# An encoder block on one core: table copies six behind each matmul group and an earlier table load; norm 2, transposes and row sums at fixed steps of the output projection

## The chip, the core and the metric

The kernel runs on one core of a Trainium2 chip. The metric is the device time of one execution in microseconds (us): the median of several runs. The engines of the core work side by side, each through its own list of instructions in order: TensorE (PE in the profile; PEld is its weight load), VectorE (DVE), ScalarE (ACT), GpSimd (POOL) and SyncE (SP, which here only issues DMAs; ACT issues a few as well). They wait for one another by semaphores.

## What is computed

One layer of an encoder block on 1024 tokens of 1024 channels, all in float32:

```python
h = rms_norm(x, norm1_g[l])
z = h @ w_in[l]                                   # 1024 -> 2560
a, gate, q, k, v = jnp.split(z, splits, axis=-1)  # 512 each
conv_out = conformer_conv(a, gate, ...)           # GLU, 31 taps, layer norm, swish
q, k = rms_norm(q), rms_norm(k)                   # per head of 64
attn_out = neighbourhood_attention(q, k, v, rpb[l])
x = x + jnp.concatenate([conv_out, attn_out], axis=-1) @ w_out[l]
h = rms_norm(x, norm2_g[l])
x = x + (jax.nn.silu(h @ w_gate[l]) * (h @ w_up[l])) @ w_down[l]   # 1024 -> 2816 -> 1024
```

The attention is over a grid of 16 rows by 64 columns: each query looks at 8 rows by 16 columns around it, clamped inside the grid, with a learned bias `rpb` by head, row offset and column offset.

## The kernel before

**Products.** A float32 product is made as three TensorE passes over operands that are split into a high and a low part (`split`, line 102: ACT casts the high part, DVE or POOL subtracts it for the low part; `mac`, line 109: high by high, high by low, low by high, lines 111 to 113). A tile of 128 tokens (or 128 features) by 512 takes 8 steps of three matmuls, one for each 128 channels.

**Order by hand.** The order of each engine's list is the order in which the Python program emits instructions. Between two steps of a product, `weave()` (line 118) takes one function off the list `woven` and calls it, so that a transpose or an evacuation lands between two steps; `unravel()` empties the list. In the first half of the kernel, `step()` (line 397) stands after each product of 24 matmuls: it calls `behind()` (line 479), which issues the next few jobs of the list `aside_dma`, then the postponed evacuation of the product before, some taps of the convolution on DVE (`pump`) and one on ACT and POOL (`side`).

**First half.** Keys (8 tiles, `wk`), GLU of the convolution (16 tiles, `gl`), queries (8 tiles, `z` from `w00` to `w03`), values (8 tiles, `z` from `w20` to `w23`). Weights are loaded by SP into three rotating buffers (`issue`, line 133, whose DMAs bear line 140) and split into their place (`take`). A value tile is copied out of PSUM by ACT and stored to DRAM, `vd` (`value_out`, line 389); windows of it come back as `vw` (`load_vw`, line 561).

**Tables.** The bias of the attention is laid out in DRAM by copies (`bias_tables`, line 444), 102 jobs in this order: for each of three types of column window, 16 runs of `rpb` into `t1` (line 461; `t<-in_rpb` in the profile) and two fills of `tf` with a very negative number (line 456; `tf<-neg`, three or four DMAs each); then 48 copies of rows from `t1` to `tf` (line 467; `tf<-t`). The list is set up after key tile 4, and from key tile 5 on each step issues four. After value tile 3 what is left is issued, and the first three tables are loaded (`table`, line 545; `tab<-tf`, line 554). The first table goes to three buffers of 1024 columns, the others to large ones that held the transposed input.

**Attention.** 32 steps, each of two heads: scores (`s`, line 581), bias and row maximum on DVE (line 594), exponential on ACT, division on POOL, transposes (`p`, line 612), product with the values (`o`, line 628). Scores of step 0 stand after value tile 5, those of step 1 after tile 6; scores and tiles share four PSUM banks.

**Output projection and norm 2.** The second column half of the output projection is made for t = 0 to 7 (lines 924 to 944, tile `pk`). After each tile: residual on DVE (`resid`, line 735), then `norm2` (line 807): store of the row to `xd`, square with sum and square root on ACT, reciprocal and product on DVE into `xn`. Of the first four tiles, `norm_T` transposes the eight channel blocks into `h2`, 3 + 2 + 3 of them woven into the products of tiles 5, 6 and 7. `t_sums` (line 832) and `s_sum` (line 882) make the sums of weight blocks and of token halves that the next stage needs; `prep` (line 848) splits the weights.

**FFN.** Gate and up projection are made as a two-by-two block scheme with seven products (m1 to m7) in place of eight, each of 4 steps, in the order m1, m2, m6, m5, m7, m4, m3 for the first two feature tiles (lines 1084 to 1091, `product` and `evac`). Its operands on the token side are A11 and A12 (from `h2`), and S1 to S4 and A22, which `s_T` (line 896) transposes from sums (`sn`) or rows (`xn`), 4 blocks each, into two PSUM tiles of 512 (`sq`, `sr`) and the two halves of one of 1024 (`sp`), and splits. `s_weave` (line 911) weaves them into the products ahead of the one that reads them. POOL makes the sums for S3 and S4 (`s_sum` with (3, 4)).

Of the kernel before, what the change touches and what calls it, by code (L numbers as in the profile page):

```python
# [7 lines left out]
F32R = mybir.dt.float32r  # L8
AF = mybir.ActivationFunctionType
# [3 lines left out]
P = 128  # L13
D = 1024
S = 1024
KB = D // P
# [50 lines left out]
def build(ctx, tc, a):  # L67
    nc = tc.nc
    pe, act, dve, pool = nc.tensor, nc.scalar, nc.vector, nc.gpsimd
# [14 lines left out]
    def H(name, dt=F32):  # L84
        return T("H", [P, 4096], 6, name, dt)
# [4 lines left out]
    def SM(name, n=8):  # L90
        return T("sm", [P, 8], 16, name)[:, :n]

    def mm(name):
        return ps.tile([P, 512], F32, tag="mm", bufs=4, name=name)

    def tp(name):
        return ps.tile([P, 512], F32, tag="tp", bufs=2, name=name)

    def cv(name):
        return ps.tile([P, 1024], F32, tag="cv", bufs=1, name=name)  # L100

    def split(hi, lo, src, sub=(pool,)):
        act.copy(hi, src)  # L103
        n = src.shape[-1] // len(sub)
        for i, eng in enumerate(sub):
            sl = slice(i * n, (i + 1) * n)
            eng.tensor_tensor(*[w[..., sl] for w in (lo, src, hi.bitcast(F32))], OP.subtract)  # L107
# [8 lines left out]
    woven = []  # L116
# [104 lines left out]
    ident = T("ident", [P, P], 1, "ident")  # L221
    ones = ST("ones")[:, :P]
    eps = T("eps", [P, 1], 1, "eps")
# [12 lines left out]
    def rstd_of(ss, scale, name):  # L236
        n = ss.shape[-1]
        sd = SM(name + "d", n)
        act.activation(sd, ss, AF.Sqrt, bias=eps, scale=scale)
        r = SM(name + "r", n)  # L240
        dve.reciprocal(r, sd)
        return r
# [4 lines left out]
    def norm_T(xs, g, dst, o, tag, lag=0, per=1, gap=0, spare=False, kbs=range(KB)):  # L247
        n = len(xs) * P

        def one(kb):  # L250
            pt = (mm if spare and kb % 3 else tp)(f"{tag}{kb}")[:, :n]
            for i, xt in enumerate(xs):
                pe.transpose(pt[:, i * P:(i + 1) * P], xt[:, kb * P:(kb + 1) * P], ident)
            hi, lo = dst[0][:, kb, o:o + n], dst[1][:, kb, o:o + n]
            if g is None:
                split(hi, lo, pt, (dve,))
            else:
                act.activation(hi, pt, AF.Copy, scale=g[:, kb:kb + 1])
                dve.scalar_tensor_tensor(lo, pt, g[:, kb:kb + 1], hi.bitcast(F32), OP.mult, OP.subtract)
        woven.extend([lambda: None] * lag)  # L260
        for k0 in range(0, len(kbs), per):
            woven.append(lambda k0=k0: [one(kbs[k0 + i]) for i in range(per)])
            woven.extend([lambda: None] * gap)
# [212 lines left out]
            for rh in range(2):  # L476
                aside_dma.extend(lambda rh=rh, ty=ty, i=i: rows_of(rh, ty, i) for i in range(8))

    def behind(n=4):
        for _ in range(n):  # L480
            if aside_dma:
                aside_dma.pop(0)()
# [62 lines left out]
    def table(rh, ty):  # L545
        n = AR * t1[ty].shape[-1]
        src = tf[rh, ty].rearrange("i j h c -> (i j) (h c)")
        if rh == 0 and ty == 0:
            parts = [(G(f"tab{k}")[:, :n * min(3, NH - 3 * k)], 3 * k) for k in range(3)]
        else:  # L550
            parts = [(H(f"tab{rh}{ty}")[:, :NH * n], 0)]
        heads = []
        for w, h0 in parts:
            nc.sync.dma_start(w, src[:, h0 * n:h0 * n + w.shape[-1]])
            heads += [w[:, o:o + n] for o in range(0, w.shape[-1], n)]
        return heads
# [90 lines left out]

    for t in range(6):
        value(t)
        if t == 3:  # L650
            while aside_dma:
                behind()
            tab[0, 0] = table(0, 0)
            tab[1, 0] = table(1, 0)
            tab[0, 3] = table(0, 2)
    pump(200)
# [17 lines left out]
    cm, x2, xn = [], {}, {}  # L674
# [69 lines left out]
    for i in range(2, 32 + 2):  # L744
# [8 lines left out]
        if i < 32:  # L753
            ss = score_mm(i)
# [45 lines left out]
    for t in range(6, 8):  # L800
# [3 lines left out]
        take(2)  # L804
        resid(t, 0, acc0[t])

    def norm2(t):
        nc.sync.dma_start(xd[t * P:(t + 1) * P, :], x2[t])
        ss = SM(f"s2{t}", 1)
        act.activation(cv(f"jk{t}"), x2[t], AF.Square, accum_out=ss)  # L810
        r = rstd_of(ss, 1.0 / D, f"r2{t}")
        xn[t] = G(f"xn{t}")
        dve.scalar_tensor_tensor(xn[t], x2[t], r, g2b, OP.mult, OP.mult)

# [6 lines left out]
    HK, QF = KB // 2, FB // 2  # L821
    raw_gu, top, tsum = {}, {}, {}

    def load_gu(i, j):
        if i < FB:
            raw_gu[i, j] = R(f"gu{i}{j}")
            nc.sync.dma_start(raw_gu[i, j], a["gu"][ms[i], j])

    def lr(w):
        return w[:, :512], w[:, 512:]  # L830

    def t_sums(i, ns):
        (b11, b21), (b12, b22) = lr(raw_gu[i, 0]), lr(raw_gu[i, 1])
        for n in ns:
            if n in (1, 3):
                tsum[i, n // 2] = G(f"ts{i}{n}")
            o = lr(tsum[i, (n - 1) // 2])[(n - 1) % 2]
            l, r = ((b12, b11), (b22, lr(tsum[i, 0])[0]), (b22, b12), (b21, lr(tsum[i, 0])[1]))[n - 1]
            dve.tensor_tensor(o, l, r, OP.subtract)  # L839
# [37 lines left out]


    h2 = []
    sn, sop, slot = {}, {}, []  # L880

    def s_sum(t, ns, eng):
        (x11, x12), (x21, x22) = lr(xn[t]), lr(xn[t + 4])
        for n in ns:
            if n == 1:
                sn[t] = G(f"sn{t}")
            s1, s2 = lr(sn[t])
            o, l, r, op = ((s1, x21, x22, OP.add), (s2, s1, x11, OP.subtract),
                           (x21, x11, x21, OP.subtract), (x12, x12, s2, OP.subtract))[n - 1]
            eng.tensor_tensor(o, l, r, op)  # L890

    def s_rows(n, t):
        return {"S1": lambda: sn[t][:, :512], "S2": lambda: sn[t][:, 512:], "S3": lambda: xn[t + 4][:, :512],
                "S4": lambda: xn[t][:, 512:], "A22": lambda: xn[t + 4][:, 512:]}[n]()

    def s_T(n, kb):
        if kb == 0:
            if n == "S4":
                q = [lr(G(f"S4{i}", F32R)) for i in range(HK)]
                sop[n] = [[w[h] for w in q] for h in range(2)]  # L900
            else:
                q = H(n, F32R).rearrange("p (w k s) -> p w k s", w=2, s=512)
                sop[n] = [[q[:, h, i] for i in range(HK)] for h in range(2)]
        if not slot:
            slot.extend([tp("sq"), tp("sr"), *lr(cv("sp"))])
        pt = slot.pop(0)
        for t in range(4):
            pe.transpose(pt[:, t * P:(t + 1) * P], s_rows(n, t)[:, kb * P:(kb + 1) * P], ident)
        split(sop[n][0][kb], sop[n][1][kb], pt, (dve,))

    def s_weave(n):
        if n == "S2":
            skip = lambda: None
            s2 = [lambda kb=kb: s_T(n, kb) for kb in range(HK)]
            woven.extend([skip, skip, s2[0], skip, s2[1], s2[2], s2[3]])
            return
        for kb in range(HK):
            woven.extend([lambda n=n, kb=kb: s_T(n, kb), lambda: None])

    g2b = G("g2b")  # L920
    nc.sync.dma_start(g2b, a["g2"].to_broadcast([P, D]))
    for i, j in ((0, 0), (0, 1), (1, 0)):
        load_gu(i, j)
    for t in range(8):
        acc = mm(f"pk{t}")
        proj(t, 1, acc, (4, 5, 6, 7, 0, 1, 2, 3))
        unravel()
        if t == 4:
            h2 += [H(f"h2{w}", F32R).rearrange("p (k s) -> p k s", s=512) for w in range(2)]
        if 4 <= t < 7:  # L930
            norm_T([xn[i] for i in range(4)], None, h2, 0, "t20", 3, gap=1,
                   kbs=((0, 1, 2), (3, 4), (5, 6, 7))[t - 4])
        if t == 7:
            s_sum(2, (1, 2), dve)
        resid(t, 1, acc)
        norm2(t)
        if t in (1, 2):
            t_sums(0, (2 * t - 1, 2 * t))
        if t in (3, 4):
            prep()  # L940
        if t in (5, 6):
            s_sum(t - 5, (1, 2), dve)
        if t == 5:
            prep()
    act.activation(warm, eps, AF.Silu)
    s_sum(3, (1, 2), dve)
    prep()
# [136 lines left out]
    for n, (i, p) in enumerate(products):  # L1084
        if i == 0 and p in NEXT:
            s_weave(NEXT[p])
        acc = product(i, p)
        if 2 <= n < 6:
            s_sum(n - 2, (3, 4), pool)
        evac(i, p, acc)  # L1090
        if late and p != "m4":
            late.pop(0)()
        if extra and p in ("m2", "m5", "m7", "m6"):
            extra.pop(0)()
        prep()
        if i == FB - 1 and p in ("m2",):
            for q in range(4):
                load_item(q)
        if i == FB - 1 and p in ("m5", "m7", "m3", "m4"):
            prep_items(1)  # L1100
# [53 lines left out]
    for s, p in enumerate(SEQ):  # L1154
        for k in range(QF - 2):
            n = s * QF + k
# [34 lines left out]
```

## Time and profile before

| | us |
|---|---|
| median of 3 runs | 1104.6 |
| the runs | 1103.31 to 1105.61 |
| the profiled execution | 1105.57 |
| its span, from the first to the last instruction | 1103.8 |

All lines of the profile, and all durations below, are of the one profiled execution. The numbers at the head of a line of a timeline are the start, in us from the start of the span, and the duration; then engine, line of the kernel, operation, written and read tiles, shapes and the number of instructions merged (x). A q behind the engine stands for its queue: the line tells when DMAs were issued, not when they landed. In brackets stands how long the engine was idle before, and what ended that.

### The profile page before, as it was taken

Reading aid. Unit: us, or ns where it says so; the run is one execution under the profiler, and the core shown is the slowest. Engines: PE = TensorE matmul, PEld = TensorE weight load, DVE = VectorE, ACT = ScalarE, POOL = GpSimd, SP = SyncE. Lnnn points to the kernel's source line nnn. Section 1 sums busy time; section 2 is a strip of 40 time slices with the busy share of each in tenths; the row PEclk is TensorE's granted clock in tenths of the full one; section 3 lists DMA queues with packets and bytes.
Section 4 is the critical chain, followed back from the end, with each engine's and each line's share of the span. In section 5 each row is a group of like instructions: output and inputs, shape, how many; then the busy total and the mean of one; then the engine's idle time right before and its main releaser. Section 6 shows DMA issues by size and latency. Waiting matters only on the chain.

```text
span 1103.8 us, 14180 instructions
## 1 busy us (share of the span) xinstructions
PE 1066.7 (97%) x5124; PEld 855.1 (77%) x5124; DVE 692.2 (63%) x1033; ACT 449.8 (41%) x1061; POOL 390.6 (35%) x303
## 2 busy tenths in 40 slices
PE   5999999997999999899999999999999999999997
PEld 4888888874657788678888888888888888888886
DVE  6557987782675425756465655646465577757883
ACT  5656336613776523542323222222322345433441
POOL 4025573501454122444544544454454300002220
PEclk9999999998999999999999999999999999999999
DMA  7004473046621552113313223322322479533651
GB/s 301 26 24 150 148 246 96 5 135 220 185 91 56 131 158 96 42 54 117 112 67 136 101 88 106 119 101 72 137 97 86 162 278 340 183 96 115 187 163 42
DMA packets 65495, 139.87 MB, mean 127 GB/s; under 512 B 12305, under 2 KB 18961, under 8 KB 64785
## 3 DMA queue, kind: packets, MB, share of 16 engines
q1 hardware_dynamic: 63584, 135.75, 37.2%
q10 hardware_dynamic: 1840, 3.22, 0.8%
q8 instruction: 40, 0.66, 0.2%
q14 instruction: 31, 0.25, 0.1%
HBM read 99.80 MB, written 44.76 MB: 131 GB/s over the span
## 4 chain that ended last, share of the span: by engine, by line
PE 88%; DVE 4%; ACT 3%; DMA 2%; issue 1%; SPq 1%; POOL 1%; ACTq 0%; DVEq 0%
PE B L111 5%; PE B L113 5%; PE B L112 5%; PE D L111 4%; PE D L113 4%; PE D L112 4%; PE z L111 3%; PE z L113 3%; PE z L112 3%; PE A L111 3%; PE A L113 3%; PE A L112 3%; PE gl L111 3%; PE gl L112 3%; PE gl L113 2%; PE p L612 2%
## 5 line engine op out<-in xcount | busy, mean ns | idle before, releaser
L314 DVE SCALAR_TENSOR_TENSOR cv<-u,par,cv 128x1009 f32<-128x1009 f32 (+11 forms) x96 | 122.7, 1278 | 2.8
L107 DVE TENSOR_TENSOR op<-sr,op 128x512 fp32r<-128x512 f32 x77 | 59.3, 770 | 15.5 <-ACT op L103 15.3
L103 ACT CAST op<-sr 128x512 fp32r<-128x512 f32 x77 | 47.6, 618 | 50.5 <-PE B2d L113 20.9
L340 POOL TENSOR_TENSOR pa<-pa,pr 128x1022 f32<-128x1022 f32 (+4 forms) x20 | 48.0, 2398 | 56.2 <-ACT pr L339 52.4
L978 DVE TENSOR_TENSOR g<-B,g 128x512 f32<-128x512 f32 x22 | 15.2, 691 | 80.3 <-PE B L113 80.3
L1146 POOL TENSOR_TENSOR ou<-ou,resm 128x512 f32<-128x512 f32 x8 | 13.3, 1665 | 141.8 <-DMA resm<-xd 141.2
L987 ACT ACTIVATE D<-D 128x512 f32<-128x512 f32 x22 | 12.8, 582 | 114.5 <-DVE D L986 114.5
L603 POOL TENSOR_SCALAR e<-e,rs 128x288 f32<-128x288 f32 (+1 forms) x64 | 34.0, 544 | 67.4 <-PE s L581 38.5
L973 DVE TENSOR_TENSOR u<-B,g 128x512 f32<-128x512 f32 x22 | 15.2, 691 | 65.2 <-PE B L113 65.2
L103 ACT CAST op<-wd 128x512 fp32r<-128x512 f32 x66 | 40.9, 619 | 33.0 <-DVE wd L1065 18.3
L107 DVE TENSOR_TENSOR op<-wd,op 128x512 fp32r<-128x512 f32 x66 | 51.7, 783 | 2.7 <-ACT op L103 1.1
L839 DVE TENSOR_TENSOR ts<-gu,ts 128x512 f32<-128x512 f32 x44 | 52.1, 1184 | 0.8
L976 ACT ACTIVATE A<-A 128x512 f32<-128x512 f32 x20 | 11.6, 582 | 77.4 <-PE A L113 77.4
L596 ACT ACTIVATE e<-e,mx 128x288 f32<-128x288 f32 (+1 forms) x64 | 36.2, 568 | 16.0 <-DVE mx L594 16.0
L594 DVE CUSTOM_DVE_ANT_0 e<-s,tab 128x288 f32<-128x288 f32 (+1 forms) x64 | 29.8, 503 | 16.6 <-DMA tab<-tf 8.4
L612 PEld LDWEIGHTS p<-ident,e 128*96 128x96 f32 (+1 forms) x192 | 20.4, 135 | 19.0 <-issue 10.7
L839 DVE TENSOR_TENSOR ts<-gu 128x512 f32<-128x512 f32 x22 | 34.2, 1553 | 0.0
L581 PE MATMUL s<-kT,qT 64*128 64x288 f32 (+1 forms) x128 | 28.6, 509 | 5.4 <-DVE mx L594 5.4
L612 PE MATMUL p<-ident,e 128*96 128x128 f32 (+1 forms) x192 | 28.1, 284 | 3.9 <-DVE pT L617 2.5
L628 PE MATMUL o<-pT,vw 96*64 96x128 f32 (+1 forms) x384 | 28.6, 283 | 1.7 <-DMA vw<-vd 1.7
L362 ACT ACTIVATE sq<-z 128x64 f32<-128x64 f32 x128 | 26.4, 247 | 8.4 <-PE z L113 8.4
L628 PEld LDWEIGHTS o<-pT,vw 96*64 96x64 f32 (+1 forms) x384 | 20.6, 138 | 7.9 <-issue 5.8
(1072 smaller groups left out, 3486.0 us busy)
## 6 DMA issues: line engine op xcount, KB each, us to landing
gu<-in_gu SPq DMA_DIRECT2D x44, 512.0 KB
sr<-sd SPq DMA_DIRECT2D x77, 256.0 KB
sd<-sd SPq DMA_DIRECT2D x22, 512.0 KB
wd<-in_wd SPq DMA_DIRECT2D x44, 256.0 KB
sd<-g SPq DMA_DIRECT2D x33, 256.0 KB
x<-in_x SPq DMA_DIRECT2D x16, 512.0 KB
xd<-x SPq DMA_DIRECT2D x8, 512.0 KB
resm<-xd SPq DMA_DIRECT2D x16, 256.0 KB
```

Source lines behind the costliest of these rows:

```text
L103: act.copy(hi, src)
L107: eng.tensor_tensor(*[w[..., sl] for w in (lo, src, hi.bitcast(F32))], OP.subtract)
L111: pe.matmul(acc, lh, rh, start=start, stop=False, skip_group_check=True)
L112: pe.matmul(acc, lh, rl, start=False, stop=False, skip_group_check=True)
L113: pe.matmul(acc, ll, rh, start=False, stop=stop, skip_group_check=True)
L314: dve.scalar_tensor_tensor(acc[:, o], uc[:, i], dwk[:, c, t:t + 1], acc[:, o], OP.mult, OP.add)
L340: pool.tensor_tensor(pa[:, o], pa[:, o], pr[:, o], OP.add)
L596: act.activation(e[:, hh], e[:, hh], AF.Exp, bias=mx, scale=-1.0, accum_out=rs[:, hh:hh + 1])
L603: pool.tensor_scalar(es[i][:, hh], es[i][:, hh], rs[:, hh:hh + 1], 1.0, op0=OP.mult, op1=OP.mult)
L612: pe.transpose(pt[:m, g * P:(g + 1) * P], es[i][:, hh, g * m:(g + 1) * m], ident)
L628: pe.matmul(os_[s_][hh * HD:(hh + 1) * HD, hp], vw[cb, rh + g][:, c:c + HD], pTs[i][:, g, hh], start=g == 0, stop=g == 2)
L839: dve.tensor_tensor(o, l, r, OP.subtract)
```

## The change

- `behind` issues six jobs in place of four.
- The remaining jobs and the first table's load stand after value tile 2 and not 3; the other two tables stay after tile 3.
- `norm2` is cut in two: store, square and root stay after the tile; reciprocal and product (`norm2_out`) stand at step 4 of the next tile.
- The transposes into `h2` stand at fixed steps: blocks 0, 1, 2 at steps 0, 2, 5 of tile 5, blocks 3, 4, 5 at the same steps of tile 6, blocks 6 and 7 at steps 0 and 1 of tile 7. `h2` is allocated ahead of the loop.
- `t_sums` of the first weights move from behind tiles 1 and 2 to step 5 of tiles 2 and 3; the row sums from behind tiles 5 and 6 and ahead of residual 7 to steps 1 of tile 6, and 2 and 6 of tile 7.
- `s_T` takes three parts for an operand: blocks 0 and 1 each to a tile `sq`, blocks 2 and 3 together to the two halves of `sp`, split by one ACT and one DVE instruction of 1024 columns (S4: by two each).
- POOL's sums: one per product behind products 1 to 8, first the four for S3, then the four for S4, in place of two behind each of products 2 to 5.

```diff
-    def behind(n=4):
+    def behind(n=6):
...
     for t in range(6):
         value(t)
-        if t == 3:
+        if t == 2:
             while aside_dma:
                 behind()
             tab[0, 0] = table(0, 0)
+        if t == 3:
             tab[1, 0] = table(1, 0)
             tab[0, 3] = table(0, 2)
...
         ss = SM(f"s2{t}", 1)
         act.activation(cv(f"jk{t}"), x2[t], AF.Square, accum_out=ss)
-        r = rstd_of(ss, 1.0 / D, f"r2{t}")
+        sd2[t] = SM(f"r2{t}d", 1)
+        act.activation(sd2[t], ss, AF.Sqrt, bias=eps, scale=1.0 / D)
+
+    def norm2_out(t):
+        r = SM(f"r2{t}r", 1)
+        dve.reciprocal(r, sd2[t])
         xn[t] = G(f"xn{t}")
         dve.scalar_tensor_tensor(xn[t], x2[t], r, g2b, OP.mult, OP.mult)
...
-        pt = slot.pop(0)
-        for t in range(4):
-            pe.transpose(pt[:, t * P:(t + 1) * P], s_rows(n, t)[:, kb * P:(kb + 1) * P], ident)
-        split(sop[n][0][kb], sop[n][1][kb], pt, (dve,))
+        two = kb == 2
+        pt = cv("sp") if two else tp("sq")
+        for j in range(1 + two):
+            for t in range(4):
+                pe.transpose(pt[:, j * 512 + t * P:j * 512 + (t + 1) * P],
+                             s_rows(n, t)[:, (kb + j) * P:(kb + j + 1) * P], ident)
+        if two and n != "S4":
+            split(*[w[:, kb:kb + 2].rearrange("p k s -> p (k s)") for w in sop[n, "all"]], pt, (dve,))
+        else:
+            for j in range(1 + two):
+                split(sop[n][0][kb + j], sop[n][1][kb + j], lr(pt)[j] if two else pt, (dve,))
 
     def s_weave(n):
...
+        skip = lambda: None
+        parts = [lambda kb=kb: s_T(n, kb) for kb in range(3)]
+        woven.extend([skip, skip, parts[0], skip, parts[1], parts[2]] if n == "S2" else
+                     [parts[0], skip, parts[1], skip, parts[2]])
...
+    beside = {t: {4: [lambda t=t: norm2_out(t - 1)]} for t in range(1, 8)}
+    for t in (2, 3):
+        beside[t][5] = [lambda t=t: t_sums(0, (2 * t - 3, 2 * t - 2))]
+    for t, s, kbs in ((5, 0, (0, 1, 2)), (6, 0, (3, 4, 5)), (7, 0, (6, 7))):
+        for n, kb in enumerate(kbs):
+            at_ = n if t == 7 else 2 * n + (n == 2)
+            beside[t].setdefault(at_, []).append(lambda kb=kb: t2_one(kb))
+    beside[6].setdefault(1, []).append(lambda: s_sum(0, (1, 2), dve))
+    beside[7].setdefault(2, []).append(lambda: s_sum(1, (1, 2), dve))
+    beside[7].setdefault(6, []).append(lambda: s_sum(2, (1, 2), dve))
+
+    def t2_one(kb):
+        mark = len(woven)
+        norm_T([xn[i] for i in range(4)], None, h2, 0, "t20", kbs=(kb,))
+        woven.pop(mark)()
+
     for t in range(8):
+        for n in range(KB):
+            woven.append(lambda fs=beside.get(t, {}).get(n, ()): [f() for f in fs])
         acc = mm(f"pk{t}")
         proj(t, 1, acc, (4, 5, 6, 7, 0, 1, 2, 3))
         unravel()
-        if t == 4:
-            h2 += [H(f"h2{w}", F32R).rearrange("p (k s) -> p k s", s=512) for w in range(2)]
-        if 4 <= t < 7:
-            norm_T([xn[i] for i in range(4)], None, h2, 0, "t20", 3, gap=1,
-                   kbs=((0, 1, 2), (3, 4), (5, 6, 7))[t - 4])
-        if t == 7:
-            s_sum(2, (1, 2), dve)
         resid(t, 1, acc)
         norm2(t)
-        if t in (1, 2):
-            t_sums(0, (2 * t - 1, 2 * t))
-        if t in (3, 4):
+        if t in (3, 4, 5):
             prep()
-        if t in (5, 6):
-            s_sum(t - 5, (1, 2), dve)
-        if t == 5:
-            prep()
+    norm2_out(7)
     act.activation(warm, eps, AF.Silu)
     s_sum(3, (1, 2), dve)
     prep()
...
-        if 2 <= n < 6:
-            s_sum(n - 2, (3, 4), pool)
+        if 1 <= n < 9:
+            s_sum((n - 1) % 4, (3 + (n > 4),), pool)
```

More of the change, by code (lines that the diff above doesn't have):

```diff
@@ L805, in build @@
         resid(t, 0, acc0[t])
+    sd2 = {}
     def norm2(t):
@@ L879, in build @@
     h2 = []
-    sn, sop, slot = {}, {}, []
+    sn, sop = {}, {}
     def s_sum(t, ns, eng):
@@ L903, in s_T @@
                 sop[n] = [[q[:, h, i] for i in range(HK)] for h in range(2)]
-        if not slot:
-            slot.extend([tp("sq"), tp("sr"), *lr(cv("sp"))])
-        pt = slot.pop(0)
-        for t in range(4):
-            pe.transpose(pt[:, t * P:(t + 1) * P], s_rows(n, t)[:, kb * P:(kb + 1) * P], ident)
-        split(sop[n][0][kb], sop[n][1][kb], pt, (dve,))
-    def s_weave(n):
[L912 to L918, printed above, removed]
+                sop[n, "all"] = [q[:, h] for h in range(2)]
+        two = kb == 2
[9 more added lines that the diff above has]
+                split(sop[n][0][kb + j], sop[n][1][kb + j], lr(pt)[j] if two else pt, (dve,))
+    def s_weave(n):
+        skip = lambda: None
+        parts = [lambda kb=kb: s_T(n, kb) for kb in range(3)]
+        woven.extend([skip, skip, parts[0], skip, parts[1], parts[2]] if n == "S2" else
+                     [parts[0], skip, parts[1], skip, parts[2]])
     g2b = G("g2b")
@@ L923, in build @@
         load_gu(i, j)
+    h2 += [H(f"h2{w}", F32R).rearrange("p (k s) -> p k s", s=512) for w in range(2)]
+    beside = {t: {4: [lambda t=t: norm2_out(t - 1)]} for t in range(1, 8)}
[12 more added lines that the diff above has]
+        woven.pop(mark)()
     for t in range(8):
+        for n in range(KB):
+            woven.append(lambda fs=beside.get(t, {}).get(n, ()): [f() for f in fs])
         acc = mm(f"pk{t}")
```

## The prediction

> **What bounds the kernel now.** I read the page first, then the waits of TensorE, then the two places where they lie.
>
> ```profile
> span 1103.8 us, 14180 instructions
> PE 1066.7 (97%) x5124; PEld 855.1 (77%) x5124; DVE 692.2 (63%) x1033; ACT 449.8 (41%) x1061; POOL 390.6 (35%) x303
> ...
> PE s L581 <- DVE mx L594: 5.4, 1, 5.4
> ```
>
> PE is busy for 1066.7 of 1103.8 us, so only some 37 us can be won by removing waits. Two stretches matter, by stage windows (length, then busy time of PE, PEld, DVE, ACT, POOL, the granted clock, DMA):
>
> ```profile
> 105.00:245.00 140.00, 140.00 (x623) 113.23 (x622) 119.03 (x108) 63.14 (x198) 66.02 (x31) 1.00 0.40 124
> 245.00:275.00 30.00, 22.27 (x118) 14.83 (x117) 7.64 (x33) 8.65 (x27) 4.93 (x10) 0.83 0.62 213
> 397.78:496.35 98.57, 91.39 (x449) 73.48 (x448) 56.37 (x77) 40.49 (x75) 32.68 (x23) 1.00 0.19 71
> ```
>
> From 105 to 245 PE never stops: the first edit can win nothing there, and can only lose. It wins, if at all, from 245 to 275, where attention starts: 7.7 us idle, and a clock of 0.83. The other edits lie in 397.78 to 496.35 (eight tiles of output projection, then ten products): 7.2 us idle.
>
> **Part 1: table copies.** What ended the idle time at 247 to 255, in the queue of SyncE (start, duration, times):
>
> ```profile
> 79.41 5.57 SPq L461 DMA_DIRECT2D t<-in_rpb  x8
> 130.00 0.34 SPq L140 DMA_DIRECT2D w02r<-in_qkv  x1
> 144.62 7.25 SPq L456 DMA_DIRECT2D tf<-neg  x8
> 160.81 5.01 SPq L467 DMA_DIRECT2D tf<-t  x8
> 185.29 43.27 SPq L467 DMA_DIRECT2D tf<-t  x8
> 232.99 16.02 SPq L467 DMA_DIRECT2D tf<-t  x14
> 249.11 2.53 SPq L554 DMA_DIRECT2D tab<-tf  x5
> 251.73 20.35 SPq L566 DMA_DIRECT2D vw<-vd  x8
> ...
> SPq L467 <- DMA vd<-vs: 48.9, 5, 34.8
> ...
> 243.66 1.23 DVE L319 TENSOR_TENSOR u<-cv,pa 128x1024 f32<-128x1024 f32 x1
> 253.33 0.46 DVE L594 CUSTOM_DVE_ANT_0 e<-s,tab 128x288 f32<-128x288 f32 x1 [8.44 <-DMA tab<-tf]
> ...
> 253.15 15.29 DMA vw<-vd
> ```
>
> Eight row copies take 5.01 us (160.81), but the next 22 took until 249.01: they waited 48.9 us for five stores of value tiles that they don't read. In the compiled program before, every DMA of SP and ACT signals one of eight semaphores, handed out in turn, and waits for the DMA eight places earlier; these 22 stand among the stores. So the tables were issued at 249.11, DVE, free at 244.89, waited 8.44 us for the first, and a vw copy issued behind five tables landed only after 15.29 us.
>
> With six per step, the 102 jobs, which start at key tile 5, are used up after 17 steps (3 key tiles, 12 GLU tiles, 2 query tiles), not 26. Then all copies are issued by about 165: from 79.4, 48 runs by 0.67 (5.57 over 8, with the gap between two), 20 fills by 0.93 (7.25 over 8, rounded up), 48 rows by 0.64, and 6 us of weight loads make 88 us. The value stores come far later: the wait of 34.8 us, from about 189, tells that an early one landed at 224. In the scheduler's order, too, the copies then stand before the first store. The first table waits for its buffers alone (they hold query weights and a partial product of the convolution, in use until some time between 206 and 213) and can be issued at about 213, the tables for the lower rows and the right edge after value tile 3, about 230. All of it is landed before 244.89, when DVE is free. DVE stays the last releaser: 244.89 plus two times 0.46 gives 245.8, before PE wants a score buffer again at 248. What follows in PE:
>
> ```profile
> 241.94:247.72 5.78, 5.78 (x26) 4.43 (x24) 2.81 (x3) 0.01 (x1) 0.00 (x0) 1.00 0.43 122
> 255.10:262.46 7.36, 7.36 (x25) 5.61 (x24) 0.98 (x6) 1.49 (x5) 1.97 (x4) 0.76 0.83 327
> ...
> 262.46 0.76 PE L581 MATMUL s<-kT,qT 64*128 64x288 f32 x4
> 263.94 0.76 PE L581 MATMUL s<-kT,qT 64*128 64x288 f32 x4
> 268.85 1.33 PE L581 MATMUL s<-kT,qT 64*128 64x288 f32 x4
> 272.67 0.76 PE L581 MATMUL s<-kT,qT 64*128 64x288 f32 x4
> 274.95 0.76 PE L581 MATMUL s<-kT,qT 64*128 64x288 f32 x4
> ```
>
> Value tile 7 starts at 248.45 (scores from 247.72, 0.73 for the two) and not at 255.10: 6.65 us. It takes 5.78 as tile 6 did, not 7.36 at a clock of 0.76: 1.6. The two attention steps from 263.94 and 268.85 took 4.91 and 3.82; the next takes 2.28 (272.67 to 274.95), for the vw copies then meet no tables: 2.6 and 1.5. **Sum 12.4, taken as 12.** Below, the least that seems likely is 5 (first rival); above, 13, since DVE's 244.89 isn't touched.
>
> What pays: weight loads behind more copies. In the new order 48 runs, 20 fills and 18 rows stand ahead of w02r, which is issued at about 143.7 and not 130.0.
>
> ```profile
> 147.10 2.41 POOL L107 TENSOR_TENSOR w02l<-w02r,w02h 128x1024 fp32r<-128x1024 f32 x1
> 159.25 0.39 PE L111 MATMUL z<-w00h,hT 128*128 128x512 f32 x1
> ```
>
> Landed by about 148, it makes its split some 3.5 us later than now, so that this ends at 153; query tile 0 wants the block at half its length, about 162. Behind the waiting cast on ACT stand the cast of w03 and the gate of a GLU tile that PE is still working on; behind POOL's part, partial products of the convolution. Cost 0, with 9 us of cover; the far end is the third rival.
>
> **Part 2: norm 2, transposes, sums.** The rows that carry it:
>
> ```profile
> 446.35 0.66 PE L253 MATMUL t<-ident,xn 128*128 128x128 f32 x4 [1.39 <-DVE h L107]
> 454.35 0.50 PE L111 MATMUL A<-h,t0m 128*128 128x512 f32 x1 [1.84 <-ACT g L970]
> 462.16 0.66 PE L908 MATMUL sp<-ident,sn 128*128 128x128 f32 x4 [1.35 <-DVE S L107]
> 473.54 0.33 PE L908 MATMUL sq<-ident,xn 128*128 128x128 f32 x1 [1.35 <-POOL xn L890]
> 495.16 0.66 PE L908 MATMUL sp<-ident,xn 128*128 128x128 f32 x4 [1.13 <-DVE S L107]
> ...
> 449.60 0.68 DVE L736 TENSOR_TENSOR x<-pk,x 128x512 f32<-128x512 f32 x1
> 450.31 1.03 ACT L810 ACTIVATE jk<-x 128x1024 f32<-128x1024 f32 x1 [2.68 <-DVE x L736]
> 451.81 1.28 ACT L945 ACT_TABLE_LOAD   x1
> 453.72 0.58 ACT L970 COPY g<-A 128x512 f32<-128x512 f32 x1
> ```
>
> The wait at 446.35 goes: blocks 6 and 7 of h are transposed at steps 0 and 1 of tile 7, six steps before product m1 wants anything. The same 24 matmuls a tile and 8 groups of transposes stay. Eight tiles of 5.46 and 8 groups at 0.45 end at about 445.1; the first two products (m1), 5.5 us, at 450.6.
>
> Now **a wait takes the place of the one removed**. m2 adds to m1's bank, so it waits for ACT's copy of it, and ACT has before it the whole norm 2 of tile 7, the table load and a cast: from residual 7 (449.60) to the end of the copy (454.30) 4.70 us, none of which the change shortens. Residual 7 now stands on DVE behind the subtractions of blocks 6 and 7 (these behind ACT's square and root of tile 6), four sums and norm 2's product of tile 6:
>
> ```profile
> 437.03 1.78 DVE L890 TENSOR_TENSOR sn<-xn 128x512 f32<-128x512 f32 x1
> 438.85 0.69 DVE L890 TENSOR_TENSOR sn<-sn,xn 128x512 f32<-128x512 f32 x1
> 443.08 1.28 DVE L813 SCALAR_TENSOR_TENSOR xn<-x,r26r,g2b 128x1024 f32<-128x1024 f32 x1
> ```
>
> Residual 6 at about 440, 1.6 for square and root, two casts and the subtraction to 444.3, four sums by 0.65 and product with reciprocal 1.5: residual 7 at about 448.7 (448.1 to 449.3). The copy ends 4.7 later, at 453.4. So m2 starts at 453.4 instead of 454.35: the tiles end earlier, and nearly all of it is given back, 0.9 us stay.
>
> [...]
>
> ```profile
> 454.35:496.35 42.00, 38.05 (x200) 30.06 (x201) 25.22 (x33) 19.11 (x35) 26.04 (x20) 1.00 0.12 38
> ```
>
> Behind it the gains stay. From m2 to m3 it took 42.0, 3.95 of it idle. The last two transpose groups of an operand now go to both halves of one tile and are read together, so the waits at 462.16 and 495.16 go (2.5). GpSimd's four sums for S3 stand ahead of the four for S4, so the 1.35 at 473.54 goes. The remaining 0.1 of idle time goes with them, and 0.15 at each of five stops, where PE loses its overlap (a matmul shows 0.4 but follows its forerunner at 0.23): 4.7 in all. Five double groups cost about 0.1 less each than two: 0.5. What is new is the wide evacuation (1024 long on ACT and DVE, as L319's 1.23) that m6's third block wants about 3.2 us after its transposes: ACT 1.0, DVE 1.25 and handing over 0.4 make 2.7, but DVE has t_sums in front of it: 0 to 1, taken 0.1. **Sum of part 2: 0.9 + 4.7 + 0.5 − 0.1 = 6.0**; below 2.5 (second rival), above 8.5 (no wait at m2).
>
> The rest (h2's buffers taken earlier, a reciprocal alone on DVE, norm 2 out at step 4 of tiles 1 to 4, before anything reads it at tile 5) costs nothing: DVE is busy 56 of 99 us there. From 496 on PE is busy nearly throughout, so a shift arrives at the end.
>
> **Sum.** The profiled execution took 1105.6 us, 1.8 beside its span, and lies 1.0 above the median of the runs, 1104.6. 1105.6 − 12 − 6 = 1087.6, on the median's scale 1086.6; I say 1087.
>
> **The rivals.**
>
> 1. The tables still come behind value stores. If the copies keep their places among the stores, tables go at 244.0 at best, when the fifth wait ended, land as now 4.2 later, and vw copies queue behind them. Value tile 7 starts 5.6 earlier, but PE then waits for vw: about 5 won, 1094. For it: 34.8 us of one wait; against: the copies have 50 us of room before the first store. Chance 0.12.
>
> 2. DVE's backlog in tiles 6 and 7 is 1.5 us longer, and m2 waits 4.4: part 2 is then 4.5, and 2.9 if PE runs slowly behind such a wait, as value tile 7 did (7.36 and not 5.78, at 0.76, after 5.37 us idle): 1090. [...] Chance 0.12.
>
> 3. **Slower**: the weights of the queries starve behind copies. Price: PE waits one for one once w02r is over 9 us later than reckoned; to eat 18 it must be 27 later, 0.32 us more on each of the 86 copies ahead of it (half as much again). Were each 1.5 times as long (62 us in all, half of it more), w02r would come 31 later: 1087 + 22 = 1109. For it: the copies come without the pauses of now; against: 8 rows in a row kept 0.63, 9 us behind eight fills. Chance 0.07.
>
> 4. Better: DVE gets residual 7 through as PE ends tile 7; no wait at m2: 1084. Chance 0.09.
>
> My forecast keeps 0.60. The range 1082 to 1096 takes in rivals 1, 2 and 4 with the bounds (5 to 13, 2.5 to 8.5), and leaves out rival 3 and the tails. About 0.2% is what a measurement tells from no change: faster 0.91, same 0.02, slower 0.07.
>
> **What would show it.** First table issued near 213, no wait of DVE for tab, no 5.4 wait at s, window 245 to 275 at a clock near 1.0; w02r issued near 144, PE still 140 of 140 busy before 245; no waits at t, sp or sq<-xn; one wait of some 3 us at A for ACT's copy, with residual 7 about 3.6 us after tile 7's last matmul. Wrong would prove me: row copies still waiting for vd, PE idle near 160, or m2 without a wait.

## The result and the profile after

| | before | after |
|---|---|---|
| median of 4 runs, us | 1105.1 | 1088.2 |
| the runs | 1103.3 to 1107.0 | 1086.8 to 1088.7 |
| the profiled execution | 1105.57 | 1088.29 |
| its span | 1103.8 | 1086.6 |

The ratio is 0.9845, interval 0.9826 to 0.9864: 1.55% faster, 17.3 us between the two profiled executions. First the head of the page after, then the wait of PE that matters below (us in total, times, the longest):

```profile
span 1086.6 us, 14172 instructions
PE 1061.7 (98%) x5124; PEld 853.6 (79%) x5124; DVE 692.0 (64%) x1029; ACT 449.1 (41%) x1057; POOL 389.5 (36%) x303
```

```profile
...
PE A L111 <- ACT g L989: 2.0, 1, 2.0
```

The waits at s, o, t, sp and sq<-xn are gone. One stays, that of m2 for ACT's copy (`A L111`): 1.84 before, 1.95 now, where the forecast had some 3. But PE is also 5.0 us less busy (1061.7 against 1066.7) with the same 5124 matmuls: stretches at half clock have gone as well (251.75 to 258.57 and 268.81 to 272.22 in the kernel before, at 0.50). The stage windows after (length, then busy time of PE, PEld, DVE, ACT, POOL, the granted clock, DMA):

```profile
105.00:245.00 140.00, 140.00 (x624) 113.18 (x623) 119.12 (x109) 63.20 (x198) 65.95 (x31) 1.00 0.50 159
245.00:275.00 30.00, 28.93 (x228) 19.86 (x226) 15.38 (x64) 16.91 (x53) 9.86 (x20) 1.00 0.47 137
385.89:479.18 93.29, 91.34 (x449) 75.29 (x448) 55.04 (x73) 39.13 (x70) 31.36 (x23) 0.98 0.19 69
441.00:479.18 38.18, 38.18 (x200) 31.78 (x201) 24.98 (x29) 18.13 (x30) 26.23 (x20) 0.96 0.13 42
```

The first is as full as before. The second is busy for 28.93 us and not 22.27, at a clock of 1.00 and not 0.83. The third, from the first matmul of `pk` (the output projection) to the first of m3, is 93.29 and not 98.57 long. The fourth, from m2 on, should stand out: no idle time at all, and yet the clock is 0.96.

**Where part 1 shows.** The queue of SyncE, then PE and DVE (start, duration):

```profile
144.45 0.53 SPq L140 DMA_DIRECT2D w02r<-in_qkv  x1
...
162.76 3.73 SPq L467 DMA_DIRECT2D tf<-t  x6
...
206.42 24.14 SPq L554 DMA_DIRECT2D tab<-tf  x5
230.66 29.59 SPq L566 DMA_DIRECT2D vw<-vd  x8
```

```profile
244.66 0.45 DVE L594 CUSTOM_DVE_ANT_0 e<-s,tab 128x288 f32<-128x288 f32 x1
```

```profile
248.26 0.50 PE L111 MATMUL z<-w20h,hT 128*128 128x512 f32 x1
...
254.05 0.76 PE L581 MATMUL s<-kT,qT 64*128 64x288 f32 x4
255.52 0.76 PE L581 MATMUL s<-kT,qT 64*128 64x288 f32 x4
258.46 0.76 PE L581 MATMUL s<-kT,qT 64*128 64x288 f32 x4
260.75 0.76 PE L581 MATMUL s<-kT,qT 64*128 64x288 f32 x4
```

The last row copy has gone out at 166.5, and the tables go from 206.42 to 230.56, not from 249.11. DVE comes to the first one at 244.66 and finds it there: no idle time in brackets. The scores that stood at 272.67 stand at 260.75: 11.92 us.

**Where part 2 shows.** DVE, ACT and PE around the last tile of the output projection:

```profile
434.91 0.69 DVE L898 TENSOR_TENSOR sn<-xn 128x512 f32<-128x512 f32 x1
435.64 0.69 DVE L898 TENSOR_TENSOR sn<-sn,xn 128x512 f32<-128x512 f32 x1
436.25 0.68 DVE L737 TENSOR_TENSOR x<-pk,x 128x512 f32<-128x512 f32 x1
```

```profile
436.96 1.03 ACT L813 ACTIVATE jk<-x 128x1024 f32<-128x1024 f32 x1 [5.64 <-DVE x L737]
...
438.46 1.28 ACT L964 ACT_TABLE_LOAD   x1
...
440.37 0.58 ACT L989 COPY g<-A 128x512 f32<-128x512 f32 x1
```

```profile
441.00 0.50 PE L111 MATMUL A<-h,t0m 128*128 128x512 f32 x1 [1.95 <-ACT g L989]
```

m1 begins at 433.39 (a row of the same timeline), so tile 7 is done by then; its residual starts at 436.25 behind two sums. From there the chain runs without a gap, residual, square, root, table load, cast, copy, to 440.95: 4.70 us, the length that the prediction took from before. m2 follows at 441.00.

Then comes what no wait shows. Three windows of 3.41 us behind each other, around the start of m2:

```profile
438.07:441.48 3.41, 1.46 (x7) 0.91 (x6) 2.90 (x4) 3.35 (x8) 0.94 (x1) 1.00 0.29 117
441.48:444.88 3.40, 3.40 (x11) 2.52 (x10) 3.37 (x3) 0.47 (x1) 3.40 (x3) 0.50 0.00 0
444.88:448.28 3.40, 3.40 (x23) 2.90 (x22) 1.55 (x2) 2.51 (x5) 2.12 (x3) 1.00 0.00 0
```

In the middle one the granted clock is 0.50 throughout; PE is "busy" all the time, but starts a matmul of 512 columns every 0.43 us, and every 0.23 in the window behind it (rows of the timeline; the counts in brackets, 11 and 23, hold short transposes too). Busy time is no progress where the clock has fallen.

### The profile page after: what moved, and what is told of

It is laid out like the page before. It is cut to its first block, busy times and chain, and to the rows that moved or that the text cites. A ratio compares the mean times of both kernels' runs of the same rounds, so it can differ in the third digit from the quotient of the medians.

```text
span 1086.6 us, 14172 instructions
## 1 busy us (share of the span) xinstructions
PE 1061.7 (98%) x5124; PEld 853.6 (79%) x5124; DVE 692.0 (64%) x1029; ACT 449.1 (41%) x1057; POOL 389.5 (36%) x303
## 4 chain that ended last, share of the span: by engine, by line
PE 92%; ACT 3%; DVE 3%; issue 1%; POOL 0%; DMA 0%; ACTq 0%; DVEq 0%
PE B L111 6%; PE B L113 6%; PE B L112 6%; PE z L111 4%; PE z L113 4%; PE z L112 4%; PE D L111 4%; PE D L113 4%; PE D L112 4%; PE A L111 4%; PE A L113 4%; PE A L112 4%; PE gl L111 3%; PE gl L112 3%; PE gl L113 3%; PE p L612 2%
## 5 line engine op out<-in xcount | busy, mean ns | idle before, releaser
L107 DVE TENSOR_TENSOR op<-sr,op 128x512 fp32r<-128x512 f32 x77 | 58.2, 756 | 16.4 <-ACT op L103 16.3
L603 POOL TENSOR_SCALAR e<-e,rs 128x288 f32<-128x288 f32 (+1 forms) x64 | 34.1, 546 | 55.6 <-DVE rs L601 49.5
L362 ACT ACTIVATION_READ_ACCUMULATOR sq<-z 128x1 f32 x128 | 26.3, 235 | 0.0
```

Of the source, the lines that this page charges most:

```text
L362: act.activation(sq[:, h * HD:(h + 1) * HD], z[:, h * HD:(h + 1) * HD], AF.Square, accum_out=ss[:, h:h + 1])
L603: pool.tensor_scalar(es[i][:, hh], es[i][:, hh], rs[:, hh:hh + 1], 1.0, op0=OP.mult, op1=OP.mult)
```

## The experiments

My theory at this point: part 1 is 12 us because six copies a step take the row copies out from among the value stores; part 2 is 5.3 us, and m2's wait costs twice, once by itself and once by the half clock behind it.

**One part alone.** In the kernel before:

```diff
-    def behind(n=4):
+    def behind(n=6):
...
-        if t == 3:
+        if t == 2:
             while aside_dma:
                 behind()
             tab[0, 0] = table(0, 0)
+        if t == 3:
             tab[1, 0] = table(1, 0)
```

> The kernel before with only the first part: six copies a step, the first table after value tile 2. My theory: the whole gain at the start of attention stands by itself, 12 us: first table issued near 206 to 213, no wait of 5.4 at s, value tile 7 at about 248.3; time 1093 (1092 to 1094). Rival, that the two parts share something (the earlier attention only helps because the later stages are also loosened): less than 11 us, 1095 or more.

Measured 1093.66 (1093.65 to 1093.76), ratio to before 0.9897, interval 0.9876 to 0.9917. The other half is the changed kernel with the same lines taken back:

> The changed kernel with four copies a step and the first table after value tile 3 again, so only norm 2, transposes and sums are moved. My theory: 5.3 us, as the changed kernel's own trace has it from the first matmul of pk to the first of m3: 1099.8 (1098.5 to 1101), with the wait at s of 5.4 back. Rival, parts not additive: 1102 or more, or under 1098.

Measured 1100.7 (1096.8 to 1103.2), ratio 0.9949, interval 0.993 to 0.9968; its `pk` to m3 takes 93.28 us. The two ratios make 1.03% and 0.51%, together 1.54%; both parts at once gave 1.55%. As far as intervals of about 0.2% to either side can tell, the parts add.

**Which edit of part 1.** The changed kernel with one of the two taken back, first the place of the load:

```diff
-        if t == 2:
+        if t == 3:
             while aside_dma:
                 behind()
             tab[0, 0] = table(0, 0)
-        if t == 3:
             tab[1, 0] = table(1, 0)
```

> The changed kernel with the first table's load back after value tile 3, six copies a step kept. My theory: what held the tables was that 22 row copies stood among the value stores; six a step takes them out of there, and the table's place in the program is of no account: 1088 (1087 to 1089), first table still issued near 206. Rival, that the earlier place of the load is what brings it forward: first table issued after value tile 3, near 212 to 225, and value tile 7 later; 1090 or more.

then the number of copies (`behind(n=4)`, the load left after value tile 2):

> The changed kernel with four copies a step again, but the first table's load and the rest of the copies after value tile 2. My theory: 14 row copies still stand behind the last value stores, SP is held until they land, tables go at about 244 to 249: 1100 (1098 to 1101). Rival, that the early place of the load brings the gain: 1088 to 1091, first table issued before 235.

Measured 1087.82 (1086.9 to 1088.3) and 1098.65 (1097.5 to 1103.1). The queue of SyncE in the first, then in the second:

```profile
206.49 24.16 SPq L554 DMA_DIRECT2D tab<-tf  x5
```

```profile
185.21 43.24 SPq L467 DMA_DIRECT2D tf<-t  x8
...
232.91 16.04 SPq L467 DMA_DIRECT2D tf<-t  x14
249.04 2.77 SPq L554 DMA_DIRECT2D tab<-tf  x5
```

With six a step the table goes at 206.49 wherever the load stands; with four, an earlier load brings the table no earlier (249.04), and SP is held for 43 and 16 us at the row copies as before; its time lies 2 us under that of the run with neither edit of part 1 (1100.7), inside the spread of both. The earlier load, which the change names, is worth nothing that these runs can tell. The number of copies is the whole of part 1.

**What more copies a step cost.** `behind(n=8)` and `behind(n=12)` in the changed kernel put more copies ahead of the weight loads:

> The changed kernel with eight copies a step. This prices the slower rival of the prediction, weights of the queries behind copies: w02r then stands behind 16 to 20 more copies and is issued at about 160 and not 144, lands by 164, its split ends at about 166.5, and query tile 0 wants it at 161.9: PE waits about 4.6, and 1 more for w03: 1094 (1092 to 1097). If the copies had room (copies run faster when they are not spread, or the splits come sooner): 1088, no wait of PE near 160.

> The changed kernel with twelve copies a step. ag03r is then issued at about 142 (now 113) and w00r at about 159 (now 122): PE waits some 7 us for ag03 in the GLU tiles and 4 to 5 for w01 to w03 in query tile 0: 1100 (1096 to 1104). If copies and weight loads do not stand in each other's way: 1088.

Measured 1097.75 (ratio to before 0.9945, interval 0.9927 to 0.9963) and 1104.6 (1.0001, 0.9987 to 1.0015). PE with eight, then with twelve:

```profile
168.29 0.80 PE L111 MATMUL z<-w02h,hT 128*128 128x512 f32 x1 [6.04 <-ACT w02h L103]
170.72 0.80 PE L112 MATMUL z<-w02l,hT 128*128 128x512 f32 x1 [1.63 <-POOL pa L335]
```

```profile
149.53 0.80 PE L111 MATMUL gl<-hT,ag03h 128*128 128x512 f32 x1 [6.68 <-ACT ag03h L103]
151.97 0.79 PE L113 MATMUL gl<-hT,ag03l 128*128 128x512 f32 x1 [1.23 <-POOL ag03l L107]
172.04 0.80 PE L111 MATMUL z<-w00h,hT 128*128 128x512 f32 x1 [2.11 <-ACT sg L429]
178.68 0.64 PE L112 MATMUL z<-w02l,hT 128*128 128x512 f32 x1 [1.80 <-POOL pa L335]
```

The places were right, both sums too low: 9.5 and 16.4 us lost against the changed kernel, where I had 5.6 and 11.5. With eight, w02r was issued at 161.20:

```profile
161.20 0.53 SPq L140 DMA_DIRECT2D w02r<-in_qkv  x1
```

PE waited 7.67 us and not 5.6; with twelve it waited 11.8 us. Clock comes on top. In windows of eight a step:

```profile
164.10:167.50 3.40, 0.00 (x0) 0.00 (x0) 1.72 (x2) 0.31 (x1) 0.00 (x0) 1.00 0.98 346
167.50:170.91 3.41, 0.98 (x2) 0.48 (x3) 0.16 (x1) 3.41 (x5) 2.59 (x3) 0.50 0.79 243
170.91:174.33 3.42, 3.42 (x9) 2.60 (x10) 3.35 (x4) 2.81 (x3) 3.42 (x2) 0.50 0.58 189
```

PE runs for 4.4 us at half speed, 2.2 us lost. Against that, no half clock follows m2 in this execution, which saves the 1.3 that it costs in the changed kernel (priced below): 7.67 + 2.2 − 1.3 = 8.6 of the 9.0 between the two profiled executions. With twelve the trace has half clock from 148.17 to 154.99, 172.06 to 175.48 and 178.89 to 182.30, with 11.1 us of busy PE in it, 5.5 lost, and none behind m2: 11.8 + 5.5 − 1.3 = 16.0 of 17.0. So six a step is no safe number: two more give back most of part 1, six more all of what the change won.

**Which edits of part 2.** The changed kernel with `s_T` and `s_weave` of before (four parts, two tiles and the halves of a third):

> The changed kernel with the four parts of an operand in sq, sr and the two halves of sp again, as before the change; all else as changed. My theory: the waits at sp come back (1.35 and 1.13 in the kernel before, with 0.15 of lost overlap at each) and the 0.1 for each of five double groups goes: plus 2.5 to 3.3, 1091 (1090.5 to 1091.5). Rival, that those waits were caused by the sums or norm 2 standing late and are gone anyway: 1088.3.

Measured 1093.11 (1091.7 to 1093.3): plus 4.9, more than either theory. The waits of PE:

```profile
441.20 0.50 PE L111 MATMUL A<-h,t0m 128*128 128x512 f32 x1 [1.98 <-ACT g L986]
449.98 0.66 PE L916 MATMUL sp<-ident,sn 128*128 128x128 f32 x4 [2.33 <-DVE S L107]
482.93 0.66 PE L916 MATMUL sp<-ident,xn 128*128 128x128 f32 x4 [1.19 <-DVE S L107]
```

The waits at sp come back, the first as 2.33 and not 1.35. PE reaches it as soon behind the start of m2 as in the kernel before (6.45 us, 6.46 before). What is late is DVE: the sum in front of its splits (`ts<-gu,ts`, 444.31) takes 1.67 beside one of GpSimd's sums, which the change has put earlier (443.68), and not 0.69 as in the kernel before (457.46). A half-clock stretch follows the wait (451.31 to 454.72). So the 4.9 is the price of four parts under the new order of GpSimd, not of the double groups alone. And GpSimd's sums in pairs again:

```diff
-        if 1 <= n < 9:
-            s_sum((n - 1) % 4, (3 + (n > 4),), pool)
+        if 2 <= n < 6:
+            s_sum(n - 2, (3, 4), pool)
```

> The changed kernel with GpSimd's sums two behind each of products 2 to 5 again (S3 and S4 of one row block together). My theory: the wait of the transposes for S3 on GpSimd comes back: plus 1.3 to 1.5, 1089.6; the first S3 transpose waits for POOL 1.3. Rival, that GpSimd, starting at product 2 and not 1, is so much later now that PE runs further ahead: plus 3 or more; or that nothing comes back: 1088.2.

Measured 1091.09 (1090.2 to 1091.9). The wait comes back with 1.70, and in the profiled execution (1090.2) `pk` to m3 takes 95.21 us, 1.9 more than in the changed kernel:

```profile
460.28 0.33 PE L917 MATMUL sq<-ident,xn 128*128 128x128 f32 x1 [1.70 <-POOL xn L898]
```

PE comes to it 0.35 sooner behind m2 than in the kernel before (17.49 and 17.84), and GpSimd is done at the same 19.19. Two of the four runs took 1.6 longer than the other two; no trace shows why, so the median, 2.9 above the changed kernel, is not explained in full.

Norm 2 cut in two, the fixed places of the transposes and the moved sums of DVE had no run of their own, but for the place of two sums in the next run; what each is worth stays open.

**The wait at m2.** Three kernels. First residual 7 ahead of two sums:

```diff
-    beside[7].setdefault(6, []).append(lambda: s_sum(2, (1, 2), dve))
...
         norm2(t)
+        if t == 7:
+            s_sum(2, (1, 2), dve)
```

> The changed kernel with DVE's two sums that stand ahead of residual 7 moved behind it. Residual 7 starts at 434.9 and not 436.25, so ACT's copy for m2 ends 1.35 earlier: the wait at m2 is about 0.7 and not 2.0. Theory A: the slow clock from 441 to 445 (0.57, 1.7 us lost) is a consequence of that wait, and both go: minus 1.3 minus 1.7, 1085.2 (1084.7 to 1085.8), clock 1.00 behind m2. Theory B: the slow clock has another cause and stays: 1086.9.

Measured 1085.42 (1085.30 to 1085.74), ratio to before 0.9825, interval 0.9805 to 0.9845. Theory A had 1085.2, theory B 1086.9. PE, and the window from m2 to m3:

```profile
439.50 0.50 PE L111 MATMUL A<-h,t0m 128*128 128x512 f32 x1 [0.50 <-ACT g L990]
```

```profile
439.50:476.37 36.87, 36.87 (x200) 30.62 (x201) 25.48 (x29) 17.94 (x30) 26.29 (x20) 1.00 0.13 44
```

The wait is 1.45 shorter, the way from m2 to m3 1.31 shorter (36.87 against 38.18) at a clock of 1.00: behind this wait of 0.50 the half clock did not come. This version beats both kernels. Next, the Silu table's load behind the copies as well:

```diff
-    act.activation(warm, eps, AF.Silu)
...
         evac(i, p, acc)
+        if n == 1:
+            act.activation(warm, eps, AF.Silu)
```

> As the run with residual 7 first, and the load of the Silu table behind ACT's two copies of m1's banks in place of ahead of them. The copies then stand 1.5 earlier on ACT: no wait at m2 at all, 1084.5 (1083.8 to 1085.2) by theory A, 1086.2 by theory B. Rival: the table load now stands in front of the casts of S2 and brings a wait of 0.5 to 1.5 in the products behind: 1085.5.

Measured 1085.64 (1084.4 to 1085.8): no gain over the run before. The wait at m2 is gone, and another has its place, though not at the casts that the rival named but at the sums ahead of S2's transposes; PE, then DVE in the run before and in this one:

```profile
442.19 0.33 PE L917 MATMUL sq<-ident,sn 128*128 128x128 f32 x1 [0.52 <-DVE sn L898]
```

```profile
438.49 0.69 DVE L898 TENSOR_TENSOR sn<-xn 128x512 f32<-128x512 f32 x1
439.21 1.65 DVE L898 TENSOR_TENSOR sn<-sn,xn 128x512 f32<-128x512 f32 x1
```

```profile
438.77 1.67 DVE L898 TENSOR_TENSOR sn<-xn 128x512 f32<-128x512 f32 x1
440.47 1.67 DVE L898 TENSOR_TENSOR sn<-sn,xn 128x512 f32<-128x512 f32 x1
```

In the run before, GpSimd's first split of the new stage started at 439.04, and only the second sum ran beside it; now it starts at 437.80, and both sums take 1.67. The kernel before shows the same: such a sum took 1.78 beside a subtraction of GpSimd (437.03), the next, behind the subtraction's end, 0.69 (438.85). The price is 1 us for each sum. Last, the wait made longer:

```diff
     norm2_out(7)
+    act.activation(cv("jkx"), x2[7], AF.Square, accum_out=SM("s2x", 1))
     act.activation(warm, eps, AF.Silu)
```

> The changed kernel with one more square with sum of row block 7 on ACT (1.03 and 0.19, into a tile that nobody reads) ahead of the Silu table's load, so that the wait at m2 is about 3.3 and not 2.0. Theory A, a wait of about 2 us already costs the whole slow stretch: plus 1.3, 1089.5, slow for about 4 us behind m2 in every run. Theory C, the slow stretch grows with the wait: plus 2 to 3, 1090.5 to 1091. Theory B, the slow stretch has nothing to do with the wait: plus 1.3, and the slow stretch stays at the same time or is missing.

Measured 1088.48 (1089.23, 1087.61, 1089.47, 1087.73); the profiled execution is the first. PE, and its windows:

```profile
442.05 0.80 PE L111 MATMUL A<-h,t0m 128*128 128x512 f32 x1 [2.99 <-ACT g L990]
```

```profile
438.66:442.06 3.40, 0.41 (x3) 0.01 (x1) 3.27 (x5) 3.37 (x7) 0.47 (x1) 1.00 0.12 46
442.06:445.47 3.41, 3.41 (x8) 2.74 (x9) 1.64 (x1) 1.56 (x3) 3.41 (x3) 0.50 0.00 0
```

The wait is 1.04 longer, the slow stretch again 3.41, and from m2 to m3 (480.22, a row of its timeline) it takes 38.17 as in the changed kernel: the price of the half clock did not grow with the wait, against theory C. But "in every run" was wrong: two of the four runs took 1.6 less, and their mean clock is 0.998 and not 0.997. Whether the stretch comes at all differs from run to run. The same shows in the eight runs of the changed kernel and of the one with the load after tile 3: five took 1088.2 to 1088.7 at a mean clock of 0.997, three 1086.8 to 1087.4 at 0.999. That these three had no slow stretch is argued from the mean clock, not seen in a timeline. Two other traces show it missing behind the same wait (last section).

## Why the prediction was right, and where it was not

- **PE full until 245, w02r with room.** Right: 140.00 of 140.00; w02r at 144.45, forecast 143.7. The last row copy went out at 166.49; the prediction's terms add up to 167.4, where it says "about 165". Eight a step tests the 9 us of cover: w02r goes 17.5 later than reckoned (161.20), by the price of the slower rival a wait of 8.5; PE waited 7.67, of which 1.63 were for a product of the convolution on POOL (`pa`). The cover is about right, and that rival's price lacked the half clock behind the wait.
- **Part 1, 12.** Right: 11.92. Value tile 7 starts 6.84 earlier (forecast 6.65), runs at full clock (1.57; forecast 1.6), the two attention steps gain 1.97 and 1.53 (2.6 and 1.5). The first table went at 206.42 and not 213: of the span in which its buffers come free I had taken the late end. Nothing hung on it, for DVE wants the table at 244.66. What carried it, the copies' place among the value stores, is shown by four and six a step with the load moved; that the load's own place is worth nothing I had not said.
- **m2's wait takes the place of the removed one.** The chain is right (4.70 us from residual 7 to the copy's end), the size is not. The two products of m1 were to end 1.9 us earlier (counted from the first `pk` matmul), of which the wait was to eat 1.0. They ended 1.57 earlier, and the wait grew by only 0.11, from 1.84 to 1.95. Residual 7 stood 50.36 us after the first `pk` matmul, forecast 50.9; m2 started 55.11 after it, forecast 55.6, before 56.57: 1.46 won, not 0.9. The four sums ahead of residual 7, counted at 0.65, took 0.68 to 0.69 each, with GpSimd idle (0.00 busy from 430 to 437); no such sum in the traces of the two kernels took less than 0.68.
- **The gains behind m2.** 4.7, 0.5 and −0.1 make 5.1; measured 3.82 (42.00 to 38.18). The failed step is the clock: I charged my own wait, about 3 us, nothing for half clock behind it, and gave that cost to the second rival alone, behind a wait of 4.4; no run shows a length of wait that parts the two. A wait of 1.95 was enough here; with eight and with twelve copies a step the same 1.95 cost nothing more. So the length of one wait, by which I had judged, is not what decides (last section). Without the slow stretch, with residual 7 first, m2 to m3 takes 36.87: 5.13, as forecast. That the sum agrees to 0.03 is in part luck, for its shares are less sure: taking the double groups back cost 4.9 and not the 2.5 to 3.3 expected, GpSimd's order 1.9 in the timeline and not 1.3 to 1.5; the two act on each other.
- **Sum.** 11.92 and 5.28 make 17.2 of the 17.28 between the profiled executions; the forecast was 18. The difference is the half clock (minus 1.3) and the earlier m2 (plus 0.5).

## What to carry to other kernels

When a queue is held, look at what it is queued behind, not only at what is waited for: here two more copies a step let 22 transfers pass ahead of the stores and were worth 12 us, while moving the load that seemed late was worth nothing, and two more again cost 9.5 because weights stood behind the copies. When a wait moves to a new place, price the clock behind it too; a window with no idle time and a granted clock below 1 (here 38.18 of 38.18 us busy at 0.96, against 36.87 at 1.00) holds lost time that no list of waits shows. And the cheapest further gain was an order: the one instruction that a chain hangs on goes ahead of work that nobody waits for yet.

## What the chip showed that I had not expected

In these traces the half clock came in pieces of 3.41 us, alone or two behind each other, at 0.50 from edge to edge. The edges in the kernel before, 251.75, 258.57, 268.81 and 272.22, lie 6.82, 10.24 and 3.41 apart: two, three and one of 3.41. Counted back from the edge of a slow piece, the time falls into windows of 3.41 us, and the clock of one window can be set beside the busy time of PE in the one ahead of it. After windows with 0.00 and 0.98 (eight a step; the second itself at half clock), 0.41 (longer wait), 1.33 (four parts, 447.90 to 451.31) and 1.46 busy (changed kernel) it was 0.50. In between lie these, of the kernel with four parts and of the kernel before:

```profile
437.66:441.07 3.41, 1.56 (x7) 0.94 (x5) 2.29 (x4) 3.35 (x8) 0.33 (x1) 1.00 0.39 154
```

```profile
265.40:268.81 3.41, 1.66 (x18) 1.10 (x18) 1.68 (x7) 1.74 (x7) 1.73 (x4) 1.00 0.19 70
```

After 1.56 the clock stayed at 1.00; after 1.66 it fell (0.50 from 268.81 to 272.22). So there is no sharp bound in busy time. In the traces of the kernel before and of the changed one, between the start-up and the last products, the windows at full clock with 0.14 (248.34 to 251.75), 1.46 and 1.66 busy were followed by a slow one; all others held 2.0 or more and were not. What decides in between, these traces do not show.

So it counted here how a wait fell into the windows. In the changed kernel the wait of 1.95 at m2 lies within one (438.07 to 441.48). With eight copies a step PE waits the same 1.95 at m2, from 449.39 to 451.34, but an edge at 450.81 divides it; the window before that edge, then m2 to m3:

```profile
447.40:450.81 3.41, 1.99 (x9) 1.32 (x7) 1.93 (x3) 3.35 (x7) 0.00 (x0) 1.00 0.38 154
451.34:488.22 36.88, 36.88 (x201) 30.64 (x201) 25.47 (x29) 17.94 (x30) 26.28 (x20) 1.00 0.12 44
```

No half clock, and 36.88 from m2 to m3, as with the wait of 0.50; with twelve a step it is 36.88 as well. The wait of 1.98 with four parts was cut at 441.07 into 1.85 and 0.13 and cost nothing more either. And with the copies alone changed, a wait of 1.83 at m2 was followed by half clock (443.13 to 446.55), though the kernel before waits 1.84 there without it; m2 to m3 took 42.03 and not 42.00 even so, since the later waits at sp and sq shrank from 3.8 to 2.3 us: the half clock cost nothing there, where idle time behind it took it up.
